# Instance norm per channel: 4 MB units of 32 KB rows become 6 MB units of 48 KB rows

## The chip, the cores and the metric

The kernel runs on one core of one Trainium2 chip. The metric is device time in microseconds (us) for one launch; the kernel before has a median of 627.53 us over 3 runs (627.28 to 627.58).

## The reference

The input `x` holds 4 x 8 x 16 = 512 channels of 256 x 256 = 65,536 float32 values (134.2 MB); the output has the same size.

```python
mu = x.mean(axis=(3, 4), keepdims=True)
var = ((x - mu) ** 2).mean(axis=(3, 4), keepdims=True)
x_norm = (x - mu) / np.sqrt(var + 1e-5)
out = x_norm * gamma[None, :, :, None, None]
```

So each channel needs its sum, its sum of squares, and then one pass of (x - mean) x scale, where scale is gamma / sqrt(var + 1e-5). `gamma` has 128 values, one for each of the 8 x 16 channels of an image, and repeats over the 4 images.

## The kernel before

**Tiling.** The flat input is cut into 32 units of 4 MB. A unit is 16 whole channels laid over 128 partitions, 8 partitions to a channel, so that each partition holds one row of 8192 contiguous values (32 KB). Every row belongs to exactly one channel.

**Staging.** Six slots `xt0` to `xt5` of 32 KB a partition hold the units in flight. A unit is loaded into its slot, reduced there, normalized in place and stored from there. The first six loads are issued at once (L56, L57): units 1 and 3 on the queue of the scalar engine (ACT), the other four on that of the sync engine (SP). After that the load of unit u + 6 is issued on SP (L141), where it waits until the store of unit u has landed, since both use one slot. All stores are issued by ACT (L139). The 16 DMA engines of the core serve both queues.

**Work of a unit**, in program order on each engine:
- VectorE sums the row (L106) while ScalarE squares it with an accumulator (L107); both results stand side by side in `st`.
- TensorE multiplies `st` by `navg` (L115), a 128 x 128 matrix that is -1/65536 inside each block of 8 partitions: every partition gets minus its channel's mean, and minus its mean square.
- VectorE forms minus the variance (L116), ScalarE takes the root (L120), VectorE the reciprocal and the product with gamma (L124, L126).
- VectorE normalizes the row (L135, `tensor_scalar`: add the negated mean, multiply by scale). In unit 0 alone ScalarE takes 3 of 8 parts of it (L132).
- ACT issues the store, which waits for the normalization; ACT's squares of the next unit come behind it.

**Set-up.** GpSimd issues two small DMAs (L54 writes 16 short rows of the output's first unit, L55 reads gamma) and builds `navg`. VectorE spreads gamma (L80), eight small matmuls turn it into a column a partition (L85, L91). In VectorE's order this stands ahead of the first L106.

The instruction order is the program's own (`manual_schedule`); the waits come from the data and the slots.

Of the kernel before, what the change touches and what calls it, by code (L numbers as in the profile page):

```python
# [1 line left out]

# [4 lines left out]

F32 = mybir.dt.float32
U8 = mybir.dt.uint8
ALU = mybir.AluOpType  # L10
ACTF = mybir.ActivationFunctionType
AX = mybir.AxisListType


@with_exitstack
def kernel(
    ctx: ExitStack,
    tc: tile.TileContext,
    x: bass.AP,
    gamma: bass.AP,  # L20
    out: bass.AP,
):
    nc = tc.nc
    B, G, C, H, W = x.shape
    P = nc.NUM_PARTITIONS
    HW = H * W
    n_ch = B * G * C
    S = 8
    K = P // S
    F = HW // S  # L30
    U = n_ch // K
    NG = (G * C) // K
    AHEAD = 6
    assert HW % S == 0 and (G * C) % K == 0

    xv = x.rearrange("b g c h w -> (b g c h w)").rearrange("(u p f) -> u p f", p=P, f=F)
    ov = out.rearrange("b g c h w -> (b g c h w)").rearrange("(u p f) -> u p f", p=P, f=F)
    gv = gamma.rearrange("g c -> (g c)")

    data = ctx.enter_context(tc.tile_pool(name="data", bufs=1))  # L40
    singles = ctx.enter_context(tc.tile_pool(name="singles", bufs=1))
    psum = ctx.enter_context(tc.tile_pool(name="psum", bufs=4, space=bass.MemoryType.PSUM))
    ctx.enter_context(tc.manual_schedule())

    slots = [data.tile([P, F], F32, name=f"xt{i}") for i in range(AHEAD)]

    def load(u, queue):
        queue.dma_start(out=slots[u % AHEAD][:], in_=xv[u])  # L48


    g_row = singles.tile([1, G * C], F32, name="g_row")
    touch = singles.tile([16, 128], F32, name="touch")
    nc.vector.memset(touch[:], 0.0)  # L53
    nc.gpsimd.dma_start(out=ov[0][0::S, 0:128], in_=touch[:])  # L54
    nc.gpsimd.dma_start(out=g_row[:], in_=gv[None, :])  # L55
    for u in range(AHEAD):  # L56
        load(u, nc.scalar if u in (1, 3) else nc.sync)  # L57

    eps_t = singles.tile([P, 1], F32, name="eps_t")
    nc.gpsimd.memset(eps_t[:], 1e-5)  # L60
    one = singles.tile([1, 1], F32, name="one")
    nc.gpsimd.memset(one[:], 1.0)
    navg = singles.tile([P, K, S], F32, name="navg")
    nc.gpsimd.memset(navg[:], -1.0 / HW)  # L64
    nc.gpsimd.affine_select(  # L65
        out=navg[:], in_=navg[:], pattern=[[-S, K], [0, S]], compare_op=ALU.is_ge,
        fill=0.0, base=0, channel_multiplier=1,
    )
    nc.gpsimd.affine_select(  # L69
        out=navg[:], in_=navg[:], pattern=[[S, K], [0, S]], compare_op=ALU.is_ge,  # L70
        fill=0.0, base=S - 1, channel_multiplier=-1,
    )
    navg_w = navg[:].rearrange("p k s -> p (k s)")
    root_eps = singles.tile([P, 1], F32, name="root_eps")
    nc.scalar.activation(out=root_eps[:], in_=eps_t[:], func=ACTF.Sqrt)  # L75
    g_rep = singles.tile([1, NG, K, S], F32, name="g_rep")
    g_ps = psum.tile([P, NG], F32, name="g_ps", bufs=1)
    g_col = singles.tile([P, NG], F32, name="g_col")

    nc.vector.tensor_copy(  # L80
        out=g_rep[:],
        in_=g_row[:].rearrange("o (n k) -> o n k", n=NG).unsqueeze(3).to_broadcast([1, NG, K, S]),
    )
    for n in range(NG):
        nc.tensor.matmul(  # L85
            out=g_ps[:, n : n + 1],
            lhsT=g_rep[:, n].rearrange("o k s -> o (k s)"),
            rhs=one[:],
            start=True, stop=True,
        )  # L90
    nc.vector.tensor_copy(out=g_col[:], in_=g_ps[:])  # L91

    junk = singles.tile([P, F], U8, name="junk")

    st = singles.tile([P, U, 2], F32, name="st")
    nvar = singles.tile([P, U], F32, name="nvar")
    std = singles.tile([P, U], F32, name="std")
    rstd = singles.tile([P, U], F32, name="rstd")
    scale = singles.tile([P, U], F32, name="scale")

    shift = singles.tile([P, 1], F32, name="shift")

    squares = []
    for u in range(U):
        t = slots[u % AHEAD]
        nc.vector.reduce_sum(out=st[:, u, 0:1], in_=t[:], axis=AX.X)  # L106
        square = nc.scalar.activation(  # L107
            out=junk[:], in_=t[:], func=ACTF.Square, accum_out=st[:, u, 1:2],
        )
        if u:  # L110

            tc.declare_no_dep(square.ins, squares[-1].ins, reason="junk, ordered by the root between")
        squares.append(square)
        ps = psum.tile([P, 2], F32, name="ps")
        nc.tensor.matmul(out=ps[:], lhsT=navg_w, rhs=st[:, u], start=True, stop=True)  # L115
        nc.vector.tensor_scalar(  # L116
            out=nvar[:, u : u + 1], in0=ps[:, 0:1], scalar1=ps[:, 0:1],
            scalar2=ps[:, 1:2], op0=ALU.mult, op1=ALU.add,
        )
        nc.scalar.activation(  # L120
            out=std[:, u : u + 1], in_=nvar[:, u : u + 1], func=ACTF.Sqrt,
            bias=eps_t[:], scale=-1.0,
        )
        nc.vector.reciprocal(out=rstd[:, u : u + 1], in_=std[:, u : u + 1])  # L124
        g = u % NG
        nc.vector.tensor_mul(  # L126
            out=scale[:, u : u + 1], in0=rstd[:, u : u + 1], in1=g_col[:, g : g + 1],
        )
        cut = F * 5 // 8 if u == 0 else F
        if cut < F:  # L130
            nc.vector.tensor_mul(out=shift[:], in0=ps[:, 0:1], in1=scale[:, u : u + 1])  # L131
            nc.scalar.activation(  # L132
                out=t[:, cut:], in_=t[:, cut:], func=ACTF.Identity, bias=shift[:], scale=scale[:, u : u + 1],
            )
        nc.vector.tensor_scalar(  # L135
            out=t[:, :cut], in0=t[:, :cut], scalar1=ps[:, 0:1], scalar2=scale[:, u : u + 1],
            op0=ALU.add, op1=ALU.mult,
        )
        nc.scalar.dma_start(out=ov[u], in_=t[:])  # L139
        if u + AHEAD < U:  # L140
            load(u + AHEAD, nc.sync)  # L141


# [1 line left out]
_INS = ['x', 'gamma']  # L145
_OUTS = [((4, 8, 16, 256, 256), 'float32')]


# [23 lines left out]
```

## Time and profile before

| what | value |
|---|---|
| median of 3 runs | 627.53 us |
| profiled execution, first to last instruction (span) | 625.2 us |
| what the median lies above that span | 2.3 us |
| bytes moved by DMA | 268.46 MB, mean 429 GB/s over the span |
| VectorE (DVE) busy | 441.8 us, 71% |
| ScalarE (ACT) busy | 241.8 us, 39% |
| TensorE (PE) busy | 21.4 us, 3% |
| L106 sum of a row, 128x8192 | 8684 ns each |
| L107 square of a row, 128x8192 | 7030 ns each |
| L135 normalization, 128x8192 | 4550 ns each |
| store, from issue to landing | median 62.5 us |
| load, from issue to landing | median 38.5 us |

The page gives the profiled execution by its span; the 2.3 us of start and end around it are taken as they are. Busy time is work of an engine; the idle column of a group names what ended the wait ahead of it. Besides the page, the trace holds one record for each DMA packet: start, duration, bytes and queue. Queue 1 is SP's, queue 10 is ACT's, queue 0 is GpSimd's. Since packets follow one another closely on an engine, the records can be put in 16 chains, one for each DMA engine; "interval" means from the start of one packet to the start of the next in such a chain.

### The profile page before, as it was taken

The page shows a single profiled execution, that of the slowest core. Times are in us where ns is not written, and L with a number is a line of the kernel's source. Part 1 is how long each engine was busy: PE and PEld are TensorE (multiplying, and loading weights), DVE is VectorE, ACT ScalarE, POOL GpSimd, SP SyncE. Part 2 cuts the span into 40 slices and gives each one's busy share as a digit, 9 for nine tenths or more (in the row PEclk, how much of TensorE's full clock was granted, in tenths as well). Part 3 has the DMA queues.
Part 4 walks back from the last instruction along what each step waited for, and adds up shares of the span by engine and source line. Part 5 has one row for each costly group of instructions (what it writes and reads, how often), then busy time and mean ns, then how long its engine had stood idle before and what let it go on. Part 6 is the DMA issues. An engine that isn't in the chain of part 4 may idle for free.

```text
span 625.2 us, 635 instructions
## 1 busy us (share of the span) xinstructions
PE 21.4 (3%) x80; PEld 19.5 (3%) x80; DVE 441.8 (71%) x164; ACT 241.8 (39%) x99; POOL 2.4 (0%) x11
## 2 busy tenths in 40 slices
PE   0200000000000000000000000000000000000000
PEld 0200000000000000000000000000000000000000
DVE  0589999998776687666786767867668676687730
ACT  0464444444443244432344423444224442244400
POOL 1000000000000000000000000000000000000000
DMA  8999999999999999999999999999999999999998
GB/s 370 436 407 432 436 436 436 436 436 430 423 436 434 434 428 434 434 436 436 436 436 428 426 436 436 432 430 434 434 436 436 436 436 421 432 436 434 434 430 367
DMA packets 9282, 268.46 MB, mean 429 GB/s; under 512 B 1072, under 2 KB 1088, under 8 KB 1088
## 3 DMA queue, kind: packets, MB, share of 16 engines
q10 hardware_dynamic: 4896, 142.61, 52.9%
q1 hardware_dynamic: 4320, 125.83, 46.8%
q0 software_dynamic: 64, 0.01, 0.0%
q14 instruction: 2, 0.02, 0.0%
HBM read 134.22 MB, written 134.23 MB: 429 GB/s over the span
## 4 chain that ended last, share of the span: by engine, by line
another core or an unknown queue 61%; DMA 17%; DVE 15%; SPq 1%; PE 1%; issue 0%; ACT 0%
DMA xt<-in_x_dram 10%; DVE st L106 10%; DMA out_dram<-xt 8%; DVE xt L135 5%; SPq L48 1%; PE ps L115 1%; ACT std L120 0%; DVE nvar L116 0%; DVE rstd L124 0%; DVE scale L126 0%; DVE shift L131 0%
## 5 line engine op out<-in xcount | busy, mean ns | idle before, releaser
L106 DVE TENSOR_REDUCE st<-xt 128x1 f32<-128x8192 f32 x32 | 277.9, 8684 | 102.2 <-DMA xt<-in_x_dram 102.2
L107 ACT ACTIVATE junk<-xt 128x8192 uint8<-128x8192 f32 x32 | 225.0, 7030 | 272.0 <-DMA xt<-in_x_dram 233.8
L135 DVE TENSOR_SCALAR xt<-xt,ps,scale 128x8192 f32<-128x8192 f32 (+1 forms) x32 | 144.0, 4500 | 1.1
L120 ACT ACTIVATE std<-nvar,eps_t 128x1 f32<-128x1 f32 x32 | 9.4, 295 | 79.4 <-DVE nvar L116 79.4
L115 PE MATMUL ps<-st,navg 128*128 128x2 f32 x64 | 17.8, 348 | 557.3 <-DVE st L106 557.3
L115 PEld LDWEIGHTS ps<-st,navg 128*128 128x128 f32 x64 | 16.0, 310 | 559.1 <-issue 546.2
L116 DVE TENSOR_SCALAR nvar<-ps 128x1 f32<-128x1 f32 x32 | 9.2, 286 | 23.8 <-PE ps L115 23.8
L124 DVE RECIPROCAL rstd<-std 128x1 f32<-128x1 f32 x32 | 5.2, 163 | 11.6 <-ACT std L120 11.6
L80 DVE COPY g_rep<-g_row 1x1024 f32<-1x1024 f32 x1 | 0.7, 681 | 14.4 <-DMA g_row<-in_gamma_dram 14.4
L107 ACT ACTIVATION_READ_ACCUMULATOR junk<-xt 128x1 f32 x32 | 6.0, 186 | 0.0
L126 DVE TENSOR_TENSOR scale<-rstd,g_col 128x1 f32<-128x1 f32 x32 | 5.1, 158 | 1.1
L85 PE MATMUL g_ps<-one,g_rep 1*128 1x1 f32 x16 | 3.5, 347 | 16.3 <-DVE g_rep L80 16.3
L85 PEld LDWEIGHTS g_ps<-one,g_rep 1*128 1x128 f32 x16 | 3.5, 326 | 16.3 <-issue 16.3
L132 ACT ACTIVATE xt<-xt,shift,scale 128x3072 f32<-128x3072 f32 x1 | 2.9, 2947 | 0.7 <-DVE shift L131 0.7
L91 DVE COPY g_col<-g_ps 128x8 f32<-128x8 f32 x1 | 0.2, 167 | 3.7 <-PE g_ps L85 3.7
L75 ACT ACT_TABLE_LOAD x1 | 1.3, 1283 | 1.7 <-PEq L156 1.7
L53 DVE MEMSET touch<- 16x128 f32 x1 | 0.2, 165 | 0.9 <-PEq L156 0.9
L54 POOL DMA_DIRECT2D out_dram<-touch x1 | 0.6, 617 | 0.8 <-DVE touch L53 0.8
L55 POOL DMA_DIRECT2D g_row<-in_gamma_dram x1 | 0.5, 487 | 0.0
L65 POOL TENSOR_SCALAR_AFFINE_SELECT navg<-navg 128x128 f32<-128x128 f32 x1 | 0.4, 400 | 0.1
L69 POOL TENSOR_SCALAR_AFFINE_SELECT navg<-navg 128x128 f32<-128x128 f32 x1 | 0.4, 399 | 0.1
L64 POOL MEMSET navg<- 128x128 f32 x1 | 0.2, 230 | 0.0
(8 smaller groups left out, 1.0 us busy)
## 6 DMA issues: line engine op xcount, KB each, us to landing
out_dram<-xt ACTq DMA_DIRECT2D x32, 4096.0 KB, 62.5
xt<-in_x_dram SPq DMA_DIRECT2D x30, 4096.0 KB, 38.5
xt<-in_x_dram ACTq DMA_DIRECT2D x2, 4096.0 KB, 31.7
out_dram<-touch POOLq DMA_DIRECT2D x1, 8.0 KB, 9.3
g_row<-in_gamma_dram POOLq DMA_DIRECT2D x1, 0.5 KB, 13.5
```

The lines of the kernel that those rows point to most:

```text
L48: queue.dma_start(out=slots[u % AHEAD][:], in_=xv[u])
L75: nc.scalar.activation(out=root_eps[:], in_=eps_t[:], func=ACTF.Sqrt)
L85: nc.tensor.matmul(out=g_ps[:, n : n + 1], lhsT=g_rep[:, n].rearrange("o k s -> o (k s)"), rhs=one[:], start=True, stop=True,)
L106: nc.vector.reduce_sum(out=st[:, u, 0:1], in_=t[:], axis=AX.X)
L107: square = nc.scalar.activation(out=junk[:], in_=t[:], func=ACTF.Square, accum_out=st[:, u, 1:2],)
L115: nc.tensor.matmul(out=ps[:], lhsT=navg_w, rhs=st[:, u], start=True, stop=True)
L116: nc.vector.tensor_scalar(out=nvar[:, u : u + 1], in0=ps[:, 0:1], scalar1=ps[:, 0:1], scalar2=ps[:, 1:2], op0=ALU.mult, op1=ALU.add,)
L120: nc.scalar.activation(out=std[:, u : u + 1], in_=nvar[:, u : u + 1], func=ACTF.Sqrt, bias=eps_t[:], scale=-1.0,)
L124: nc.vector.reciprocal(out=rstd[:, u : u + 1], in_=std[:, u : u + 1])
L126: nc.vector.tensor_mul(out=scale[:, u : u + 1], in0=rstd[:, u : u + 1], in1=g_col[:, g : g + 1],)
L132: nc.scalar.activation(out=t[:, cut:], in_=t[:, cut:], func=ACTF.Identity, bias=shift[:], scale=scale[:, u : u + 1],)
L135: nc.vector.tensor_scalar(out=t[:, :cut], in0=t[:, :cut], scalar1=ps[:, 0:1], scalar2=scale[:, u : u + 1], op0=ALU.add, op1=ALU.mult,)
```

## The change

- **Rows of 48 KB.** The units are now 2 x 16 channels (unit 0 and unit 21, 4 MB each, as before) and 20 x 24 channels between them (6 MB, 12,288 values = 48 KB a partition). Four slots of 48 KB a partition replace six of 32 KB.
- **A row no longer belongs to one channel.** In a 6 MB unit a channel is 5 1/3 rows. A row is treated as three pieces of 4096 values, and 16 pieces make a channel. VectorE sums the three pieces with one instruction, ScalarE squares them with three. A mask `by_c` (which of three channels a piece of this partition belongs to) sorts the piece sums into three columns for each of the two values; one matmul with `navg3` (blocks of 16 partitions, 8 groups of 3 channels) averages all six columns; the mask `by_j` brings the averages back to the pieces. The normalization is one instruction a piece, with its own mean and scale.
- **Loads** are all issued on SP, whole.
- **Gamma** is copied to all partitions by one matmul, and VectorE picks each piece's value ahead of the loop (L127 to L155 of the new file); GpSimd builds four masks and `owner` in place of `navg`.
- **ScalarE helps** with the normalization in units 0, 1, 2, 20 and 21 (3/8 of a 4 MB row, the third piece of a 6 MB row).

```diff
-    S = 8
-    F = HW // S
-    AHEAD = 6
+    F = 4096
+    SLOTS = 4
+    sizes = [2] * 1 + [3] * ((n_ch - 16 * 2) // 24) + [2] * 1
+    helped = (0, 1, 2, U - 2, U - 1)
...
-    slots = [data.tile([P, F], F32, name=f"xt{i}") for i in range(AHEAD)]
+    slots = [data.tile([P, 3 * F], F32, name=f"xt{i}") for i in range(SLOTS)]
...
-    for u in range(AHEAD):
-        load(u, nc.scalar if u in (1, 3) else nc.sync)
+    for u in range(SLOTS):
+        load(u)
...
+    for b in range(8):
+        near = g_all[:, 3 * b : 3 * b + GC].rearrange("p (m k) -> p m k", k=8)[:, :, :3]
...
+            nc.vector.scalar_tensor_tensor(
+                out=g_ch[:], in0=near, scalar=in8[:, b], in1=g_ch[:], op0=ALU.mult, op1=ALU.add,
+            )
...
+        nc.vector.reduce_sum(
+            out=st[:, u, :n, 0], in_=t.rearrange("p (j f) -> p j f", j=n), axis=AX.X,
+        )
+        for j in range(n):
+            square = nc.scalar.activation(
+                out=junk[:, :step], in_=t[:, j * step : (j + 1) * step],
+                func=ACTF.Square, accum_out=st[:, u, j, 1:2],
+            )
...
+            nc.vector.tensor_mul(
+                out=parts[:],
+                in0=st[:, u].rearrange("p j v -> p v j").unsqueeze(1).to_broadcast([P, 3, 2, 3]),
+                in1=by_c[:].unsqueeze(2).to_broadcast([P, 3, 2, 3]),
+            )
+            nc.vector.reduce_sum(out=sums[:, u], in_=parts[:], axis=AX.X)
+            nc.tensor.matmul(
+                out=ps[:], lhsT=navg3, rhs=sums[:, u].rearrange("p k v -> p (k v)"),
+                start=True, stop=True,
+            )
+            nc.vector.tensor_mul(
+                out=picks[:],
...
+            nc.vector.reduce_sum(out=means[:, u], in_=picks[:], axis=AX.X)
+            mean = means[:, u, :, 0]
+            nc.vector.tensor_mul(out=nvar[:, u], in0=mean, in1=mean)
+            nc.vector.tensor_add(out=nvar[:, u], in0=nvar[:, u], in1=means[:, u, :, 1])
...
+        for j in range(n):
+            lo, hi = j * step, min((j + 1) * step, cut)
+            if lo < hi:
+                nc.vector.tensor_scalar(
+                    out=t[:, lo:hi], in0=t[:, lo:hi], scalar1=mean[:, j : j + 1],
+                    scalar2=scale[:, u, j : j + 1], op0=ALU.add, op1=ALU.mult,
+                )
+        nc.scalar.dma_start(out=rows(of, u), in_=t)
+        if u + SLOTS < U:
+            load(u + SLOTS)
```

## The prediction

> **What bounds the kernel now.** I read the page's slices first, then the chain that ended last, then the groups and the timeline of the end.
>
> The slices (40 equal parts of the span; busy tenths, then GB/s) and the DMA queues:
>
> ```profile
> DVE  0589999998776687666786767867668676687730
> DMA  8999999999999999999999999999999999999998
> GB/s 370 436 407 432 436 436 436 436 436 430 423 436 434 434 428 434 434 436 436 436 436 428 426 436 436 432 430 434 434 436 436 436 436 421 432 436 434 434 430 367
> q10 hardware_dynamic: 4896, 142.61, 52.9%
> q1 hardware_dynamic: 4320, 125.83, 46.8%
> ```
>
> The DMA engines are full in every slice but the first and last, and most slices stand at one figure, 436 GB/s; the two queues take 99.7% of the engines' time together. VectorE is full only up to 110 us.
>
> The chain (start, duration, what), in its steady part and at the end:
>
> ```profile
> 160.27 18.95 another core or an unknown queue
> 179.22 0.02 SPq L48
> 179.24 0.03 issue
> 179.27 0.33 SPq L48
> 179.60 18.97 another core or an unknown queue
> 198.57 0.02 SPq L48
> ...
> 547.05 38.49 DMA xt<-in_x_dram
> ```
>
> The chain goes from store landing to load issue to the next landing, every 198.57 - 179.22 = 19.35 us: one unit loaded and one stored, 8.39 MB. No engine stands in it. The groups say the same from the other side:
>
> ```profile
> L106 DVE TENSOR_REDUCE st<-xt 128x1 f32<-128x8192 f32 x32 | 277.9, 8684 | 102.2 <-DMA xt<-in_x_dram 102.2
> L107 ACT ACTIVATE junk<-xt 128x8192 uint8<-128x8192 f32 x32 | 225.0, 7030 | 272.0 <-DMA xt<-in_x_dram 233.8
> L80 DVE COPY g_rep<-g_row 1x1024 f32<-1x1024 f32 x1 | 0.7, 681 | 14.4 <-DMA g_row<-in_gamma_dram 14.4
> ```
>
> Both readers of the data wait for loads. The end of the timeline shows that compute is not late there either:
>
> ```profile
> 585.57 8.69 DVE L106 TENSOR_REDUCE st<-xt 128x1 f32<-128x8192 f32 x1 [4.33 <-DMA xt<-in_x_dram]
> 600.62 0.34 ACTq L139 DMA_DIRECT2D out_dram<-xt  x1
> ```
>
> The last load lands at 585.5, the last store is issued at 600.6, and DMA works until 623.9: stores of earlier units are still queued. So the time is: first packet, plus packets of one DMA engine, plus its delays, plus the close.
>
> **The DMA engine's own account.** From the packet records: each engine moves 512 packets of 32,768 B (8 rows x 32 units x 2 directions) and 64 semaphore writes of 4 B, two a unit. The interval of a 32 KB packet is 1209.4 ns, whichever queue comes next; of a 4 B one 6 ns; the sixteen 512 B packets of L54 take 27 ns, and as neighbours overlap by 3.5 ns, their interval is 23.5. Engines start at 1.8 to 2.8 us. The one that ended last: 1.95 + 512 x 1.2094 = 619.21 + about 0.40 of small packets + 2.38 of delays = 623.94; the close ends the span at 625.24, and the median stands 2.29 above. Delays are packets longer than 1213 ns: on most engines 0.4 to 0.8 us at the first packet and 0.3 to 1.2 between 39.8 and 42 us, where the first store starts; the rest, 0 to 0.9 us, is scattered, with two instruction fetches (0.25 to 0.55 us on the engines they meet).
>
> **Rows of 48 KB.** From 512 B and 32 KB: (1209.4 - 23.5) / 32,256 B = 0.036765 ns a byte, which leaves 4.7 ns a packet at zero bytes. 48 KB was never seen; this line gives 1807.1 + 4.7 = 1811.8 ns. An engine then has 20 units x 16 = 320 packets of 48 KB and 32 of 32 KB: 320 x 1.8118 + 32 x 1.2094 = 618.48, against 619.21: **-0.74 us** (160 fewer packets x 4.7 ns is the same sum). Bounds: 0, if a long packet costs half as much again, and -0.96, if each packet carries the 6 ns of the 4 B row. I take 4.7, as three sizes lie on its line. The Trainium skill, DMA: Bandwidth & Descriptors, "Why small descriptors are slow (HBM only)", speaks against any gain: it puts a fixed ~3 cycles on a packet and calls merging worth it only up to 256 B. By that this term would be 0 and the time 627.4; the rows agree that the cost is small, but 160 times 4.7 ns is still there.
>
> **Fewer DMAs.** 20 loads and stores fewer an engine: with 22 units, 44 semaphore writes for 64, 20 x 6 ns = **-0.12 us**.
>
> **Loads whole on SP.** Units 1 and 3 leave ACT's queue; four issues of 0.33 us each on SP follow at once, so the queue holds 22 MB by 2.2 us. Cost 0 if one queue of loads keeps an engine as full as two. No row shows loads alone on one queue: until 39.9 us both carry loads, later one carries stores. The nearest row is the end, stores alone on queue 10: intervals 1209.4, packet to packet and unit to unit. I take 0; the other end is a rival below.
>
> **VectorE, GpSimd, ScalarE.** These are hidden if stores reach the queue in time. A 6 MB unit on VectorE: sum 12,288 x 8684 / 8192 = 13.03 us; mask product and sum, about 0.4 (0.16 to 0.29 each by the 128x1 rows); matmul and gaps 0.7; four small products and sums 0.9; root and gaps 0.4; reciprocal and scale 0.4; three normalizations of 4096 values, 4550 / 2 = 2.28 to 2.4 each, 7.0. Sum 22.8 us, against 16 x 1.8118 + 0.012 = 29.0 us of DMA for the unit: 79% busy. ScalarE: 3 x (3.5 + 0.19) = 11.1 us of squares beside the 13.03. A store waits on ACT ahead of the next squares as before.
>
> *Opening.* Gamma landed at 15.1 us; then one matmul, and on VectorE 14 small instructions of 0.16 to 0.3 us, about 4 us with gaps; GpSimd's extra twelve selects and fills of at most 0.4 us are done by 8. So the first sum starts near 20 (22.8 before; unit 0 itself lands near 13, alone on its queue), store 0 is issued 8.7 + 4.8 later, near 33.5, store 1 near 33.5 + 22.8 - 2.3 (ScalarE's piece) = 54, store 2 near 74.5. Without store 1 the engines have 22 MB of loads and store 0: 26 / 4 x 9.675 = 62.9 us of work from 2 us on, until 65, and load 4 (14.5 us) behind store 0. Eleven us to spare.
>
> *Middle.* Four slots at 29.0 us make a turn of 116 us, as six at 19.35 do. Of it 22.8 is compute and 58 is load plus store side by side: 35 us of queue remain.
>
> *End.* When load 21 lands, unit 20 is being normalized; the last store is issued 15 us later, with a good 23 us of stores ahead of it. No idle time. ScalarE's help at both ends lies under this cover and is worth 0; without cover a piece of 2.3 us would be its price.
>
> **Sum.** 627.53 - 0.74 - 0.12 = **626.7 us** (span 624.4). The two openings and the first store stay. The scattered delays of whichever engine ends last may be 0.9 less or as much more.
>
> **Rivals.**
> *Packets cost more than the line says, or scattered delays shrink.* With 6 ns a packet (-0.96), -0.12, and 0.5 of the 0.9 us of scattered delays gone: 625.9. For it: the other 15 engines ended 0.4 us or more before the last. Against: delays fall on some engine each time.
> *A 48 KB row goes out as two packets* (the change does not do what it says): 640 + 32 = 672 packets for 512, 160 x 4.7 = +0.75, -0.12: 628.2. No row is longer than 32 KB; every row so far is one packet.
> *One queue of loads alone leaves gaps* (slower). Place: 2 to 33 us, some 21 packets an engine. The price is what a load's start adds when nothing is read ahead, 0.6 us by the first packets: 21 x 0.6 = 12.6 us, 639; it turns the result slower from 0.1 us a packet on, 2.1 us. A middle price of 0.15 us a packet gives 629.9. For it: the mix of two queues in the opening is all the trace shows. Against: stores alone on one queue have no gap. The Trainium skill, the same page, "Rules for kernel authors", states that spreading DMAs over issuing engines brings no bandwidth; by it this rival is worth 0.
> *VectorE loses its rate in L238* because mean and scale now come from one tile: at the sum's 1.06 ns a value 13.0 us for 7.0, 28.8 a unit, level with DMA. From store 1 near 58 the units follow at VectorE's pace (24.5 in units 2 and 20, 28.8 in the 17 between), so the last store goes out near 58 + 49 + 490 + 16 = 613 and lands by 624: between 627 and 629. Against: 4550 ns for 8192 in place is half the sum's time, with one operand already in SBUF.
>
> **How the numbers follow.** A measurement of this kernel tells about 0.2%, 1.25 us: 626.28 to 628.78 is the same. Forecast 0.60 (own range 626.2 to 627.6, by the bounds 0 and -0.96 and part of the delays), cheaper packets 0.20, two packets 0.05, gaps 0.12, VectorE 0.03. Faster: 0.20 and 0.05 of the forecast's low edge, 0.25. Slower: 0.12 and a third of VectorE's, 0.13. Same: the rest, 0.62. The range from 625.7 to 628.6 leaves out the gaps and a thin edge below.
>
> **What would show it.** Right: packets of 49,152 B with an interval near 1812 ns; DMA at 436 GB/s or a little over in all inner slices; a span near 624.4. Wrong: intervals over 1209 ns between 2 and 33 us; two packets a row; a slice below 400 GB/s after 60 us; sums that wait for nothing, all through.

## The result, and the profile after

The changed kernel took 628.74 us (median of 22 executions, 627.24 to 630.66), the one before 626.99 beside it (22 executions, 626.66 to 627.59): ratio 1.0027, interval 1.0021 to 1.0033. So it became slower, by 1.75 us, a little more than the 1.25 us that the prediction allowed a measurement of this kernel, where 626.7 us was forecast. Its spread changed too: 3.4 us between its shortest and longest execution, against 0.9 before. The profiled execution took 630.37 us with a span of 628.7, and is one of the longer ones. (A ratio compares means and leaves out the longest executions of a kernel where they stand far above the rest, so with a long tail it can differ from the quotient of the medians.)

The slices of the page after, and its DMA queues (packets, MB, share of 16 engines):

```profile
DVE  2999595959586685969696967768595959595770
DMA  8999999999999999999999999999999999999995
GB/s 368 450 417 450 400 451 447 403 447 450 401 450 447 403 450 447 403 450 447 403 450 447 403 450 445 407 450 444 410 444 447 410 444 444 416 438 428 439 428 248
q1 hardware_dynamic: 3168, 134.22, 49.6%
q10 hardware_dynamic: 3168, 134.22, 49.3%
q14 instruction: 4, 0.03, 0.0%
```

The swing between 400 and 450 is no stall: a packet of 48 KB is counted where it starts, and a slice of 15.7 us holds eight or nine of them on an engine (16 engines x 9 x 49,152 B in 15.7 us are 450 GB/s, with 8 they are 400). What did change is the last slice, 248 GB/s where before had 367, with its DMA digit at 5 instead of 8, and queue 14: four fetches of instructions where before had two.

Compute is as early as before, or earlier. The groups (busy, mean ns of one, then idle before it and what ended that), and three stamps of the timeline:

```profile
L178 DVE TENSOR_REDUCE st<-xt 128x3 f32<-128x12288 f32 (+1 forms) x22 | 276.4, 12564 | 119.9 <-DMA xt<-in_x_dram 119.9
L182 ACT ACTIVATE junk<-xt 128x4096 uint8<-128x4096 f32 (+1 forms) x62 | 231.1, 3727 | 261.9 <-DMA xt<-in_x_dram 258.9
L238 DVE TENSOR_SCALAR xt<-xt,means,scale 128x4096 f32<-128x4096 f32 x57 | 134.2, 2408 | 0.6
```

```profile
15.59 8.67 DVE L178 TENSOR_REDUCE st<-xt 128x1 f32<-128x8192 f32 x1
...
29.29 0.37 ACTq L242 DMA_DIRECT2D out_dram<-xt  x1
...
49.61 0.34 ACTq L242 DMA_DIRECT2D out_dram<-xt  x1
```

Both readers of the data still wait for loads, and the first store is issued at 29.3 us, 4 us ahead of the forecast.

The end shows where the time is. The DMA view for 622 to 628 us of the span, in 40 slices of 0.15 us, first before and then after (GB/s of all 16 engines together, packets):

```profile
GB/s 218 1529 437 0 218 0 0 0 0 0 0 0 0 0 0 0 0 0 0 0 0 0 0 0 109 0 0 0 0 0 0 0 0 0 0 0 0 0 0 0
q10 hardware_dynamic: 27, 0.36, 14.0%
```

```profile
GB/s 0 0 219 0 0 0 0 0 0 0 218 0 0 0 0 0 0 0 218 0 0 0 0 0 0 0 218 0 0 0 0 0 0 0 0 0 0 0 0 0
DMA packets 20, 0.13 MB, mean 22 GB/s; under 512 B 16, under 2 KB 16, under 8 KB 16
q10 hardware_dynamic: 20, 0.13, 5.2%
```

In before, eleven last packets of 32 KB start between 622 and 622.75, and everything is over by 624 (the 109 at 625.6 is a fetch on another queue, past the last instruction). In after only four packets are left, one every eight slices, 1.2 us: one behind the other on **one engine**. Put in 16 chains, the packet records say the same: 15 engines ended at 622.2 to 623.1 us, and one at 627.17; in before all lie between 622.9 and 623.94. The median engine ended 1.1 us earlier than before (622.3 and 623.4). The time is that of the slowest of the 16.

The account of that engine against the one that ended last in before, from the packet records of the two profiled executions (us; by the chain's own first packet before's start is 1.85, where the prediction had 1.95). Of the other delays only those over 70 ns are counted, so the sum stays 0.15 us short of the end:

```
                                           before    after   difference
start of the engine                          1.85     2.65     +0.80
512 of 32 KB / 320 of 48 KB + 32 of 32 KB  619.21   618.48     -0.73
semaphore writes and short packets           0.40     0.28     -0.12
stretch in the opening (to 60 us)            1.58     0.66     -0.92
instruction fetches on this engine           0.31     0.62     +0.31
stretch of the packet behind a fetch         0.54     1.07     +0.53
stretch of other packets after 60 us         0        3.26     +3.26
sum                                        623.89   627.02     +3.13
end of the engine                          623.94   627.17     +3.23
```

"Stretch" is what a packet took over the 1213 ns of 32 KB or the 1815 of 48 KB. The 3.26 us are nine loads of 0.07 to 0.69 us each and three stores (0.10 to 0.24). Ten of these twelve follow directly on a 4-byte semaphore write that closes a unit of the other queue, the other two one packet later. In the whole trace after 60 us, 25 loads were stretched by more than 20 ns, 5.3 us in sum, two of them behind fetches; in before 2, by 0.79 us, both behind a fetch. The later start and the shorter stretch in the opening (+0.80 and -0.92) nearly cancel.

### The profile page after: what moved, and what is told of

Same layout as the page of the kernel before. It is cut to its first block, busy times and chain, and to the rows that moved or that the text cites. A ratio compares the mean times of both kernels' runs of the same rounds, so it can differ in the third digit from the quotient of the medians.

```text
span 628.7 us, 717 instructions
## 1 busy us (share of the span) xinstructions
PE 13.2 (2%) x46; PEld 11.5 (2%) x46; DVE 449.3 (71%) x271; ACT 262.1 (42%) x153; POOL 5.1 (1%) x23
## 3 DMA queue, kind: packets, MB, share of 16 engines
q1 hardware_dynamic: 3168, 134.22, 49.6%
## 4 chain that ended last, share of the span: by engine, by line
DMA 68%; DVE 24%; ACT 3%; another core or an unknown queue 1%; PE 1%; issue 1%; POOL 0%; ACTq 0%; DVEq 0%; SPq 0%
DMA xt<-in_x_dram 37%; DMA out_dram<-xt 30%; DVE st L178 15%; DVE xt L238 6%; ACT junk L182 2%; DMA g_row<-in_gamma_dram 1%; PE ps L197 1%; ACT xt L231 0%; ACT std L220 0%; DVE g_ch L136 0%; DVE rstd L223 0%; DVE scale L224 0%; PE ps L212 0%; DVE parts L191 0%
## 5 line engine op out<-in xcount | busy, mean ns | idle before, releaser
L178 DVE TENSOR_REDUCE st<-xt 128x3 f32<-128x12288 f32 (+1 forms) x22 | 276.4, 12564 | 119.9 <-DMA xt<-in_x_dram 119.9
L182 ACT ACTIVATE junk<-xt 128x4096 uint8<-128x4096 f32 (+1 forms) x62 | 231.1, 3727 | 261.9 <-DMA xt<-in_x_dram 258.9
L238 DVE TENSOR_SCALAR xt<-xt,means,scale 128x4096 f32<-128x4096 f32 x57 | 134.2, 2408 | 0.6
L220 ACT ACTIVATE std<-nvar,eps_t 128x3 f32<-128x3 f32 (+1 forms) x22 | 6.5, 297 | 82.5 <-DVE nvar L209 74.8
L197 PE MATMUL ps<-sums,navg 128*128 128x6 f32 x40 | 11.3, 356 | 551.5 <-DVE sums L196 551.5
L197 PEld LDWEIGHTS ps<-sums,navg 128*128 128x128 f32 x40 | 10.0, 311 | 552.8 <-issue 507.0
L231 ACT ACTIVATE xt<-xt,shift,scale 128x4096 f32<-128x4096 f32 (+1 forms) x5 | 17.3, 3460 | 3.7 <-DVE shift L228 3.7
L238 DVE TENSOR_SCALAR xt<-xt,ps,scale 128x5120 f32<-128x5120 f32 x2 | 5.9, 2942 | 0.0
L127 DVE COPY g_all<-g_ps 128x128 f32<-128x128 f32 x1 | 0.3, 291 | 4.2 <-PE g_ps L125 4.2
L212 PE MATMUL ps<-st,navg 128*128 128x2 f32 x4 | 1.1, 348 | 31.8 <-DVE st L178 31.8
L214 DVE TENSOR_SCALAR nvar<-ps 128x1 f32<-128x1 f32 x2 | 0.6, 288 | 1.5 <-PE ps L212 1.5
(33 smaller groups left out, 12.5 us busy)
```

What stands on the lines that cost most here:

```text
L178: nc.vector.reduce_sum(out=st[:, u, :n, 0], in_=t.rearrange("p (j f) -> p j f", j=n), axis=AX.X,)
L182: square = nc.scalar.activation(out=junk[:, :step], in_=t[:, j * step : (j + 1) * step], func=ACTF.Square, accum_out=st[:, u, j, 1:2],)
L197: nc.tensor.matmul(out=ps[:], lhsT=navg3, rhs=sums[:, u].rearrange("p k v -> p (k v)"), start=True, stop=True,)
L220: nc.scalar.activation(out=std[:, u, :n], in_=nvar[:, u, :n], func=ACTF.Sqrt, bias=eps_t[:], scale=-1.0,)
L231: nc.scalar.activation(out=t[:, cut:], in_=t[:, cut:], func=ACTF.Identity, bias=shift[:, u : u + 1], scale=scale[:, u, n - 1 : n],)
L238: nc.vector.tensor_scalar(out=t[:, lo:hi], in0=t[:, lo:hi], scalar1=mean[:, j : j + 1], scalar2=scale[:, u, j : j + 1], op0=ALU.add, op1=A ...
```

## The experiments

All were run beside the kernel before; "before" below is its median in those runs. The open question was why loads are stretched now. Two words are used throughout. A **fetch** is an 8 KB packet of queue 14 on one DMA engine. The **lead** is how many MB the loads are ahead of the stores, from the packet records: in before 16.0 to 16.5 MB, in after 13.5 to 15.0 (an MB of the lead is 2^20 bytes, as in the units of 4 and 6 MB).

### First: which part of the change

**The same kernel again.**

> The changed kernel, unaltered, a second look. In its first trace 15 of the 16 DMA engines ended at 622.2 to 623.1 us, where the packet sum puts them, and one at 627.2, after 15 longer load packets (3.9 us in all) and two instruction fetches. If the delay belongs to 48 KB packets or the 48 KB pitch (length or pitch theory), one or more engines again collect 2 to 5 us of longer loads and the ratio is about 1.003. If it was the accident of one execution, all engines end within 1 us and the ratio is near 0.999.

629.44 us (12 executions, 627.28 to 631.03; before 627.09), ratio 1.0036 (1.0026 to 1.0047). The profiled execution was a short one, 627.79 us, and yet had 22 stretched loads with 5.1 us, several of them within 0.4 us of the times of the first trace (near 93.7, 106.9, 116, 145, 194 and 385 us), others not. This time they lay on several engines and the last ended at 624.6. So how much is stretched repeats; on which engine it gathers decides the time.

**Rows of 48 KB moved as two halves**, 24 KB a packet, layout and compute unchanged.

```diff
+    def halves(u):
+        n = sizes[u] * F
+        return [(0, n // 2), (n // 2, n)] if sizes[u] == 3 else [(0, n)]
...
-            nc.sync.dma_start(out=home(u)[:, cut:], in_=rows(xf, u)[:, cut:])
+            for lo, hi in halves(u):
+                nc.sync.dma_start(out=home(u)[:, lo:hi], in_=rows(xf, u)[:, lo:hi])
...
-        nc.scalar.dma_start(out=rows(of, u), in_=t)
+        for lo, hi in halves(u):
+            nc.scalar.dma_start(out=rows(of, u)[:, lo:hi], in_=t[:, lo:hi])
```

> The changed kernel with every 6 MB load and store issued as two DMAs of half rows: packets of 24 KB, the row pitch in memory still 48 KB, units and slots unchanged. Cost by the packet line: 640 packets of 908.2 ns for 320 of 1811.8, +1.5 us, and 40 more semaphore writes, +0.24 us, per engine. Length theory: the longer loads go, the last engine is back with the others, ratio to the kernel before about 1.0014. Pitch theory, or fetch theory (more instruction fetches hit one engine): they stay, ratio about 1.0055.

629.56 us (5 executions, 629.18 to 629.97), ratio 1.0039 (1.0027 to 1.0051). The only loads stretched are three behind fetches (1.3 us), at a lead of 13.4 to 14.0 MB for most of the span, near after's. The spread is 0.8 us in place of 3.4. The level is higher, also than the 1.0014 of the length theory, for known reasons in the main: 320 more packets an engine and 40 more semaphore writes are 320 x 4.7 ns + 0.24 = 1.74 us over after's sum, and the last engine met a second fetch (0.85). That leaves 0.7 of the 2.47 us over before without a name. The interval of the 24 KB packets is 908.2 ns, a fourth size on the prediction's line (4.7 + 24,576 x 0.036765 = 908.2).

**Before, with all loads on SP.**

```diff
-        load(u, nc.scalar if u in (1, 3) else nc.sync)
+        load(u, nc.sync)
```

> The kernel before with the two loads of units 1 and 3 moved from ACT's queue to SP's. All theories of the delay: ratio 1.000 (within 0.0005), no gap between load packets of one queue in the opening. If a single queue of loads left gaps, over 1.002.

632.05 us (6 executions, 629.01 to 638.69), ratio 1.0055 (1.0037 to 1.0073): a miss, and the surprise of the study. This one line of the change, priced at 0, costs more than the whole change did. The slices of its profiled execution (638.14 us):

```profile
GB/s 369 433 418 429 420 431 429 424 418 421 429 431 429 429 427 427 431 429 427 422 427 424 424 420 429 429 431 429 429 429 424 427 429 426 424 420 422 437 424 307
```

Hardly a slice reaches the 436 that most slices of before show. The opening, where the two queues of loads were traded for one, is not the place (433 and 418 there); the loss lies along the whole span. After 60 us some 1,100 packets of all 16 engines were stretched by more than 20 ns, most by 26 to 270, 131 us in sum or 8.2 an engine. (The ratio leaves out the two longest of the six executions, this one among them.) What differs from before all along is the lead: 12.5 MB, since store 0 now finds the ACT queue empty and its packets start after 25 or 26 load packets an engine, not after 33.

The Trainium skill, DMA: Bandwidth & Descriptors, "Rules for kernel authors", says that spreading DMAs over issuing engines brings no bandwidth. The prediction weighed the loads by that and by the stores alone at the end; this run is 0.55% against it, and the measurement decides. A run below shows that the rule and the number can stand together: most of the cost is not the queue's.

**Before, with four more one-column copies a unit on VectorE**, to bring more fetches.

```diff
+        for _ in range(4):
+            nc.vector.tensor_copy(out=pad[:], in_=scale[:, u : u + 1])
```

> The kernel before with four more one-column copies a unit on VectorE (128 more instructions, 0.7 us a unit, under the load waits). Fetch theory: one to three more 8 KB instruction fetches in the span, each taking 0.3 us and lengthening a load by some 0.5 us on the engine it meets, and the ratio rises by up to 0.0014 where one engine is met twice. Length and pitch theories: 1.000.

627.72 us (11 executions, 627.51 to 628.62), ratio 1.0012 (1.0003 to 1.0020). There are three fetches for two, and the packet behind each is longer by 0.25 to 0.54 us: 0.309 + 0.54 = 0.85 us for the engine that meets one. So a second fetch on one engine is a part of the loss, and at most half of it. How large a part this run does not show: its profiled execution was the longest of the eleven, and 54 stores were stretched there too, 3.2 us in sum, where before had 27 with 1.3.

### Second: fetches, queues, or the lead

**After's transfers with few VectorE instructions.** A row is handled as one piece with one group, and squares are summed over its first two thirds. So the kernel leaves out the sorting of pieces into channels, and the statistics of its 6 MB units are not those of the reference.

```diff
-        three = sizes[u] == 3
+        three = False
...
-                out=junk[:, :step], in_=t[:, j * step : (j + 1) * step],
+                out=junk[:], in_=t[:, : 2 * F],
...
-            g = sixteens.index(8 * starts[u] % GC)
+            g = 0
```

> The changed kernel's transfers with less work on VectorE: a 48 KB row is treated as one piece that belongs to one group of 8 partitions, squares are summed over its first two thirds, the normalization is one instruction; units, slots, rows, queues and the set-up stay. So the statistics of the 6 MB units are left wrong, about 100 instructions a run fall away on VectorE. Fetch theory (each 8 KB instruction fetch on VectorE's behalf takes 0.3 us and lengthens the next packet by some 0.5 us, always on one DMA engine; two of them made it the straggler, and its lag then sets off the longer loads): one such fetch or none, few longer loads, ratio 0.9985 to 0.9995. Length theory (48 KB loads are stretched whatever the program does): 3 us and more of longer loads stay, ratio 1.002 or more.

628.52 us (12 executions, 626.79 to 631.69; before 627.06), ratio 1.0027 (1.0012 to 1.0043). Two fetches, as in before; 26 stretched loads with 4.5 us, as in after. The mask arithmetic, the three normalizations and the extra fetches are not needed for the loss: the transfers of the change (48 KB rows, four slots, loads on SP) are enough.

**After with loads 1 and 3 on ACT**, as before had them.

```diff
-            nc.sync.dma_start(out=home(u)[:, cut:], in_=rows(xf, u)[:, cut:])
+            queue = nc.scalar if u in (1, 3) else nc.sync
+            queue.dma_start(out=home(u)[:, cut:], in_=rows(xf, u)[:, cut:])
```

> The changed kernel with the loads of units 1 and 3 issued on ACT, as the kernel before has them. Distance theory (what stretches packets is how far the stores' addresses lie behind the loads', 16.3 MB before, 12.5 MB in the kernel before with all loads on SP, 14.3 MB after the change; the opening sets it): the distance moves by 1 MB or more, and the longer loads go or grow at once, ratio below 1.0005 or above 1.004. Fetch and length theories: no change, 1.003.

632.17 us (6 executions, 629.86 to 634.06), ratio 1.0079 (1.0059 to 1.0099). Undoing that line of the change makes it worse: the lead grows to 15.7 to 17.3 MB (16.45 in the mean), the value that was clean with 32 KB rows, and one engine collects far more than the others (4.8 us of stretched loads, where the median engine has 0.04). About 1 us more is lost by all engines near 54 us, where loads wait for their slots and start again.

**Before with five slots**, for a lead near after's.

```diff
-    AHEAD = 6
+    AHEAD = 5
```

> The kernel before with five slots for six, its loads on both queues as they were. Distance theory: the stores' addresses come to lie 12 to 13 MB behind the loads', as in the kernel before with all loads on SP, and hundreds of packets are stretched by 0.1 to 0.4 us on all engines, ratio 1.003 to 1.01. If the stretched packets of that kernel came from the opening on one queue itself, and not from the distance: 1.000 to 1.001.

628.51 us (9 executions, 628.33 to 634.35), ratio 1.0034 (1.0016 to 1.0052). The hundreds of stretched packets that a bad lead of any kind should bring did not come: at 13.6 to 14.4 MB the stream is clean after 80 us. The loss is one of the opening: at 65 to 77 us loads wait for their slots and start again, which stretches packets by 1.4 us an engine on average.

**After with four small products of a 6 MB unit moved to GpSimd**, the whole computation kept (VectorE has 191 instructions for 271).

```diff
-            nc.vector.tensor_mul(
+            nc.gpsimd.tensor_mul(
...
-            nc.vector.tensor_mul(out=nvar[:, u], in0=mean, in1=mean)
-            nc.vector.tensor_add(out=nvar[:, u], in0=nvar[:, u], in1=means[:, u, :, 1])
+            nc.gpsimd.tensor_mul(out=nvar[:, u], in0=mean, in1=mean)
+            nc.gpsimd.tensor_add(out=nvar[:, u], in0=nvar[:, u], in1=means[:, u, :, 1])
...
-        nc.vector.tensor_mul(out=scale[:, u, :n], in0=rstd[:, u, :n], in1=gamma_u)
+        (nc.gpsimd if three else nc.vector).tensor_mul(out=scale[:, u, :n], in0=rstd[:, u, :n], in1=gamma_u)
```

> The changed kernel with five of the small products of a 6 MB unit (the parts, the two of the variance, the scale) on GpSimd, so that VectorE has 150 instructions for 230; the result is the same. Fetch theory: VectorE's fetches fall from two to one or none and lie on another DMA engine than GpSimd's, ratio 1.000 or below for 1.003. Length theory: 1.003. A rival cost: GpSimd's products take longer, but 6 us of slack a unit hide it.

628.15 us (12 executions, 627.57 to 632.08, clusters near 628 and 631), ratio 1.0032 (1.0017 to 1.0047). Two fetches still met one engine, and 19 loads were stretched by 4.8 us. It settles little beyond the two runs above.

### Third: moving the lead by a tiny load

A load of short rows on ACT ahead of store 0 (64 B a row) lets a few more load packets pass before the first store packet. It adds one to eight packets of 11 ns an engine and changes nothing else in the program.

```diff
+    filler = singles.tile([64, 16], F32, name="filler")
...
+        if u == 0:
+            nc.scalar.dma_start(out=filler[:], in_=rows(xf, 0)[:64, :16])
```

**In after, 64 rows; and in after, 16 rows.** The thought was that packets are stretched where a unit of loads and one of stores close out of step.

> The changed kernel with one tiny load (64 rows of 64 B, four packets and a semaphore write an engine) put into ACT's queue just ahead of store 0. Engines take packets of the two queues in turn, so it moves every store five turns back against the loads: in the changed kernel a store ends when the load beside it is at its third of eight rows, here load and store should end together, as in the kernel before. Seen so far: outside the fetches, nearly every stretched 48 KB packet comes right behind a semaphore write that ends one queue's unit in the middle of the other's. Boundary theory: no such packets are left, ratio 0.999 to 1.0005, a spread under 1 us. Length theory without the boundary: 20 and more stay, 1.003.

> The control for the aligned kernel: the same tiny load with 16 rows, one packet and a semaphore write an engine, which moves the stores two turns, so that the ends still do not meet. Boundary theory: stretched packets behind semaphore writes, at other row numbers than before, ratio 1.002 to 1.004. If the tiny load itself changes the time: as the aligned kernel.

64 rows: 628.05 us (12 executions, 627.52 to 633.80; before 627.16), ratio 1.0026 (1.0010 to 1.0042); 54 stretched loads, 10.4 us, 42 of them behind neither a semaphore write nor a fetch. The closes did not meet exactly, so the thought was not put to a clean test, but as it stood it does not explain this trace. 16 rows: 627.62 us (11 executions, 627.07 to 628.75), ratio 1.0009 (1.0000 to 1.0018), with **64 stretched loads and 17.3 us**, more than three times after's, and a lower time. They lay on all engines (1.1 us each on average), which ended between 623.3 and 625.1. 38 of the 64 loads stood behind neither a semaphore write nor a fetch. That is the rule of the slowest engine from the other side.

**The same 64 rows in the kernel with few VectorE instructions, and in the one with products on GpSimd.**

> The kernel with less work on VectorE (48 KB rows taken as one piece of one group, so the statistics of the 6 MB units are left wrong) with the ends of loads and stores aligned by the tiny load of 64 rows. Boundary theory: what is left is the packet sum and one instruction fetch on an engine, so the 0.86 us of the prediction show: ratio 0.9985 to 0.9995. If long loads do not come from the boundaries: 1.002 as without the tiny load.

> The whole computation, with the five small products on GpSimd and the ends aligned by the tiny load of 64 rows. Boundary theory: no stretched packets but behind fetches, ratio 0.9985 to 1.000. Length theory: 1.003.

627.63 us (11 executions, 626.47 to 635.27), ratio 1.0017 (0.9996 to 1.0039), and 627.93 us (12 executions, 627.53 to 638.44), ratio 1.0028 (1.0006 to 1.0049). The first one's profiled execution, the shortest of its eleven, is the clean case that the forecast described: 626.47 us, span 624.7 (forecast 626.7 and 624.4). Its DMA view from 622 to 628 us:

```profile
GB/s 218 0 0 0 0 0 0 0 0 0 0 0 0 0 0 0 0 0 0 0 0 0 0 0 0 0 0 0 0 0 0 0 0 0 0 0 0 0 0 0
q10 hardware_dynamic: 17, 0.03, 1.4%
```

One packet of 32 KB is left at 622.0 us, and all engines ended at 622.4 to 623.3. There the gain of the long rows is seen by itself, in one execution; the kernel's median is not below before's. The second kernel's profiled engines ended at 622.5 to 624.4, the later ones behind fetches. Both still have executions of 635 us and more. The lead is 16.4 to 17.6 MB in both, as in after with 64 rows, whose trace had 54 stretched loads: with 48 KB rows one lead gives clean and stretched executions.

### Fourth: the lead by itself

**Before with all loads on SP and 128 short rows; before with 64; after with 128.**

> The kernel before with all loads on SP, and one tiny load (128 rows of 64 B, eight packets and a semaphore write an engine) in ACT's queue ahead of store 0. With all loads on SP each engine took 25 or 26 load packets before its first store packet, 12.5 MB; in the kernel before it is 33 on every engine, 16 MB; this is to bring it back to 32 to 34. Distance theory: the stretched packets go, ratio 0.9998 to 1.001 for 1.0055, spread under 1.5 us. Queue theory (one queue of loads, or engines that start their stores at different turns, is bad whatever the distance): stays over 1.003.

> The kernel before, its loads on both queues, with the tiny load of 64 rows in ACT's queue ahead of store 0: the stores run some five turns later against the loads, 38 packets ahead for 33, and units of the two queues no longer end together. Distance theory: packets are stretched at the new distance, ratio 1.002 or more. Queue theory: the queues are as before, 1.000.

> The changed kernel with the tiny load of 128 rows ahead of store 0, so that each engine has taken 27 or 28 load packets before its first store packet, for 20. Distance theory: another number of stretched packets, ratio anywhere from 0.999 (none: the packet sum and the fetches alone) to 1.008. Length theory (48 KB loads are stretched at any distance): 1.003, with 20 to 30 of them.

Before with all loads on SP and the delay: 628.06 us (11 executions, 627.60 to 628.66; before 626.90), ratio 1.0015 (1.0007 to 1.0024), where it had been 1.0055. The lead is 14.5 to 15.2 MB, and two loads are stretched, 0.8 us. Its slices:

```profile
GB/s 369 435 402 435 435 435 433 435 435 434 435 429 433 434 431 431 429 431 435 435 433 435 433 433 435 433 435 435 431 433 435 431 431 427 431 435 435 433 435 339
```

The loads go out on the same one queue as in the run at 632.05 us, and nearly every slice is full again. So most of the cost was not that of one queue in itself but of the lead that it brings; for the 0.15% that is left the runs show no cause. Before, shifted: lead 18.1 to 18.8 MB, 627.38 us (11 executions, 627.18 to 627.82), ratio 1.0007 (0.9998 to 1.0016), clean. After, delayed: lead 16.4 MB early and 14 to 15 later, 635.88 us (11 executions, 627.56 to 639.42), ratio 1.0080 (1.0045 to 1.0115). Its windows (us of length, the five engines' busy time, clock, DMA share, GB/s):

```profile
626.00:628.00 2.00, 0.00 (x0) 0.00 (x0) 0.00 (x0) 0.00 (x0) 0.00 (x0) 1.00 0.08 33
628.00:630.00 2.00, 0.00 (x0) 0.00 (x0) 0.00 (x0) 0.00 (x0) 0.00 (x0) 1.00 0.08 33
630.00:632.00 2.00, 0.00 (x0) 0.00 (x0) 0.00 (x0) 0.00 (x0) 0.00 (x0) 1.00 0.04 16
632.00:634.00 2.00, 0.00 (x0) 0.00 (x0) 0.00 (x0) 0.00 (x0) 0.00 (x0) 1.00 0.08 33
634.00:636.00 2.00, 0.00 (x0) 0.00 (x0) 0.00 (x0) 0.00 (x0) 0.00 (x0) 1.00 0.04 16
```

A packet or two in 2 us, 0.04 to 0.08 of sixteen engines: ten microseconds in which one engine works off its rest. Fifteen engines had ended by 625.7; this one was stretched by about 12.6 us after 60 us. It is after's own loss, about three times as large (there 3.26 and the 1.07 behind fetches). This execution took 639.1 us and is one of the five longest of eleven, which the ratio leaves out; the two shortest took 627.6. The same lead of 14.5 to 16.4 MB is clean with 32 KB rows.

### Fifth: layout or length of a packet

**Halves with the delay**, for a longer lead with 24 KB packets; **only loads as halves; only stores as halves**.

> The kernel with the 6 MB transfers issued as two DMAs of half rows (24 KB packets, rows in memory still 48 KB apart, units and slots unchanged), with tiny loads of 128 and 64 rows ahead of store 0 that delay the stores to some 16 MB behind the loads, as in the delayed changed kernel, which took 635.9 us. Length theory (a 48 KB load is what gets stretched): clean, 629.2 to 630 as the half-row kernel without delay, spread under 1.5 us. Layout theory (the 48 KB pitch or the 6 MB unit at that distance): 632 and more, a spread of several us.

> The changed kernel with only the 6 MB loads cut in two DMAs of half rows; stores stay whole. 160 more packets and 20 more semaphore writes an engine, +0.87 us. Length theory for loads: few stretched packets but behind fetches, ratio 1.001 to 1.002, spread under 1.5 us. Otherwise the spread of the changed kernel stays, 627 to 631 and up. Loads and stores no longer move alike in a turn (24 KB against 48), so their distance drifts.

> The changed kernel with only the 6 MB stores cut in two; loads stay whole at 48 KB. The same +0.87 us. Length theory for loads: loads are stretched as in the changed kernel or more, ratio over 1.003, spread of 3 us and more. If it is the stores' length that matters: 1.001 to 1.002.

Halves delayed: 629.35 us (5 executions, 629.14 to 629.65; before 627.01), ratio 1.0035 (1.0022 to 1.0048). The lead is 16.6 to 17.2 MB, and beyond the fetches no load is stretched by more than 50 ns. With the first run of halves, ten executions of ten lie within 0.9 us of each other, with the layout, the slots and the compute of after. At leads of 13.5 to 17.6 MB eight traces with 48 KB loads had 19 to 104 stretched loads, and two had next to none but behind fetches. So it is not the 48 KB pitch of the rows: the long packet is needed.

Loads as halves alone: 661.04 us (6 executions, 653.14 to 666.03), ratio 1.0509 (1.0466 to 1.0552), a wide miss. Page lines of its profiled execution, queues and the chain by engine:

```profile
q1 hardware_dynamic: 6048, 134.22, 49.4%
q10 hardware_dynamic: 3168, 134.22, 49.2%
...
DVE 67%; another core or an unknown queue 22%; issue 3%; PE 2%; ACT 1%; DMA 1%; DVEq 0%; POOL 0%; ACTq 0%
```

Loads have twice the packets of stores for the same bytes. The queues take turns packet by packet, so beside stores a load gets 24 KB for each 48: its landings come late and in bursts, the lead swings from 7 to 21 MB, VectorE stands in 67% of the chain, and 810 packets are stretched by more than 20 ns, 304 us in sum. This kernel says nothing on the question it was built for.

Stores as halves alone: 627.98 us (12 executions, 627.64 to 633.98, four of them over 629.6), ratio 1.0034 (1.0014 to 1.0054). The tail stays with 48 KB loads. In its profiled execution, one of the short ones, 10 loads were stretched, 2.4 us, three of them behind fetches.

## Why the prediction was wrong, step by step

- **Rows of 48 KB, -0.74 us:** right. 48 KB packets have an interval of 1811.8 ns, the forecast's figure to the digit, one packet a row, and fewer semaphore writes gave their 0.12. The rivals "cheaper packets" and "two packets" fell by this. One reason given for 4.7 ns was not sound: two sizes made the line, and the third, the 4 B packet at 6 ns, lay 1.2 ns above it. The 24 and 48 KB rows of these runs are what bears it out.
- **VectorE, ScalarE hidden:** right. Three L238 took 7.07 us in the chain (2408 ns each by the groups), so VectorE kept its rate and that rival fell. A unit held VectorE 21.5 us of 29.06:

```profile
400.00:429.06 29.06, 0.56 (x2) 0.50 (x2) 21.46 (x13) 11.51 (x8) 0.00 (x0) 1.00 1.00 435
```

- **Opening:** off in size, without weight. Gamma landed at 10.7 us and not 15.1, so the first sum began at 15.6 for "near 20", and stores 0 and 1 were issued at 29.3 and 49.6 for 33.5 and 54.
- **End:** the cover was thinner than "a good 23 us". Load 21 was awaited until 597.9, the last store was issued 13.7 us later at 611.6, and six engines ran dry for 0.03 to 0.31 us near 612.5. They ended near 622.3, 5 us before the last one, so it cost nothing here.
- **Loads on SP, 0; rival "gaps in one queue":** the rival fell as it was put. With loads alone between 2 and 32 us the intervals are 1811.8 ns. But the 0 was wrong as a step: the place to look was not the gaps of one queue but when store 0 enters against the loads. In before that line alone is worth +0.55%, and a delay takes three quarters of it back. What it costs in the changed kernel stays open, as undoing it there made the time longer (1.0079).
- **Sum, span 624.4:** right for 15 engines and for one execution of the kernel with few VectorE instructions (624.7). Wrong for the slowest engine.
- **The step that failed** is the last term: "the scattered delays of whichever engine ends last may be 0.9 less or as much more". They were carried over from before as if every kernel had the same. They belong to the kernel: in the profiled execution 3.26 us of stretched packets that before did not have, and 0.84 for a second fetch on the same engine, less 0.92 in the opening and plus a later start (0.80). That execution is 1.6 us above the median of the 22; at the median the kernel is 1.75 us over before, where -0.86 was forecast. The forecast's own sentence "Delays fall on some engine each time" was the right lead; what it lacked was that a longer packet and another order of loads and stores change how many there are.

What is shown: 48 KB loads bring the tail (every such kernel but the one with 16 short rows had executions over 3 us above before's median, and the transfers alone, without the mask arithmetic, have it); 24 KB packets in the same layout do not; a fetch costs the engine it meets up to 0.85 us; the lead, with queue and packet size unchanged, turns the stretching on and off at 32 KB (12.5 MB bad; 13.6 to 18.8 clean). At 48 KB no such switch is shown: at one lead, and in executions of one kernel, there is both. What stays open is the mechanism inside the DMA. That the loads wait there for a place in memory that the stores use at the time was thought of, and no run tests it. The semaphore write that closes a unit cannot be the whole cause: with the 64 and the 16 short rows most stretched loads stood behind another data packet. Length alone does not explain that 32 KB rows are stretched at one lead, nor one execution of 634.35 with five slots. No version beat the kernel before; the nearest were before shifted (1.0007) and after with 16 short rows (1.0009).

## What to carry to other kernels

Where DMA bounds a kernel, the sum over packets gives the time of an average engine, but the kernel ends with the slowest of 16: put the packet records in chains, and look at the last engine and at the spread of executions before believing a gain of a few tenths of a per cent. Count delays as part of the kernel (packet length, number of instructions, when the first store enters behind the loads), not as noise that stays. Two queues that share the engines take turns by packet, so give loads and stores rows of one size.

## What the hardware showed that was not expected

- A packet costs 4.7 ns + 0.036765 ns a byte at 512 B, 24, 32 and 48 KB alike: 23.5, 908.2, 1209.4 and 1811.8 ns.
- A fetch of 8 KB takes 0.31 us of one DMA engine, and the packet behind it 0.11 to 0.54 us more. 128 more VectorE instructions brought one more.
- A semaphore write has an interval of 6 ns, and yet in the changed kernel 18 of the 23 stretched loads that are not behind a fetch stand directly behind one; with the 64 short rows it is 8 of 54. The Trainium skill, DMA: Bandwidth & Descriptors, "Anatomy of one DMA — SWDGE (gpsimd) path", calls the semaphore write itself essentially free, for DMAs that GpSimd issues. Beside the 1811.8 ns of a 48 KB packet the 6 ns of these DMAs of SP and ACT agree; the longer packets behind it are not in that price.
- The turn between two queues goes by packet whatever its size: halving the rows of loads alone took the kernel to 661 us.
